# The order of the input projections in a hybrid mLSTM and differential-attention layer

## The chip, the cores and the metric

The kernel runs on one core of a Trainium2 chip, in one launch. The metric is the device time in microseconds (us) of that core. The core's engines work side by side and each runs its own instructions in the order in which the program lists them: TensorE (PE, with its weight loads PEld), VectorE (DVE), ScalarE (ACT), GpSimd (POOL), and SyncE (SP), which here issues the transfers.

## The reference

One decoder layer over 2048 tokens of width 1024, all in float32.

```python
u = rmsnorm(h, attn_norm_g[l])
z = jnp.matmul(u, w_in[l].astype(jnp.float32))
mq, mk, mv, mo, mi, mf, aq, ak, av = split_columns(z)
y_m = mlstm_mixer(mq, mk, mv, mo, mi, mf, ...)      # 4 heads of 128, conv + gates, chunkwise memory
y_a = diff_attn_mixer(aq, ak, av, ...)              # 4 heads, two causal softmax maps per head
h = h + jnp.matmul(jnp.concatenate([y_m, y_a], axis=-1), w_out[l])
u2 = rmsnorm(h, mlp_norm_g[l])
h = h + jnp.matmul(jnp.square(jax.nn.relu(jnp.matmul(u2, w_up[l]))), w_down[l])
gate = jax.nn.sigmoid(jnp.matmul(rmsnorm(h, ple_norm_g[l]), w_ple_gate[l]))
h = h + gate * jnp.matmul(p[l], w_ple_proj[l])
```

Attention is causal, so a query block of 128 tokens needs the keys and values of all blocks before it. The mLSTM memory runs along the sequence, so a part of the sequence can only follow the part before it.

## The kernel before

The sequence is cut into four parts of 512 tokens, numbered j = 0 to 3. `phase1` (the input projections, mLSTM, attention, and the output projection of part 0) is followed by `phase2` (the rest of the layer), whose large buffer `U_r` takes space that phase 1 gives back at its end. Large products are made three times, from a high and a low part of each operand (`mm3`, lines 137 to 139, and `prod`, line 921).

The projections of one part come in two pieces: `z_attn(j)` (six weight groups: values, queries and keys of the four heads, and the gates) and `z_mlstm(j)` (eight weight groups, two a head). Each is 576 matmuls. Here they are called A0 to A3 and M0 to M3. Both read the scaled activations `Uh` and `Ul` of part j, which lie in one buffer, `ubuf`, that holds one part at a time. `make_u(j)` fills it: four loads of x (line 285), four products with the gain (line 297), four splits into high and low (lines 75 and 76). The first time for a part it also makes the row statistics (lines 290, 294, 307). `project` walks through `ORDER` and calls `make_u` whenever the part differs from that of the entry before. A piece's last K blocks leave late: `qk_prep` normalises and rotates (tile `KS_r`, line 749), and `k_out` transposes them on PE (line 756).

Attention is a second stream, one unit for each part, head and block of 128 queries, 64 in all. Unit number i of a head (0 to 15) has i + 1 key blocks, in 1 to 4 chunks of 512 keys. `attn_front` runs two sets, one for each softmax map: scores on PE (784, 787, with the mask 786), row maxima on DVE (788, 792, 793), exponentials on ACT (796); then DVE combines the two maps (808). `attn_back` transposes the result (PE 820, copies on ACT 823 and DVE 825), multiplies by the values (PE 832), and scales it (ACT 835 and 838, DVE 840, POOL 841 and 842); line 499 transposes it back and 500 copies it out. The stream may enter part j only when A(j) is done, and until then it yields:

```python
while j not in done:
    yield 0.0
```

The loop at the end of `phase1` mixes the two streams by hand-set costs: each step of projection work adds a debt of attention work, by what is left of each. A scheduler then orders the instructions once more, so that the order of the built program is not quite that in which the code was written; it stands fixed before the kernel runs.

Of the kernel before, what the change touches and what calls it, by code (L numbers as in the profile page):

```python
# [33 lines left out]
FY = 1.2  # L34
AHEAD = 1
MOVES = [(("z", "s"), ("z", "ta")), (), (("ta", "s"),), (("z", "s"),)]
ORDER = [("a", 0), ("a", 1), ("a", 2), ("m", 0), ("m", 1), ("a", 3), ("m", 2), ("m", 3)]


@with_exitstack  # L40
# [135 lines left out]
def phase1(tc, a, wbuf, ubuf, rbuf, ps, yT, hd, qkdr, vdr, ident, identr, identb, masks, ones, negh, split, rstd_col, spread, acc0):  # L176
    nc = tc.nc
    with ExitStack() as ctx:
# [78 lines left out]
        wseq, wq = [], []  # L257
        for kind, j in ORDER:
            if kind == "a":
# [9 lines left out]
        def u_front(j, tb):  # L269
            if rcol[j] is None:  # L270
                rcol[j] = pc.tile([P, 2, 4], F32, name=f"rcol{j}")
                stats.add(j)
            xk = pu.tile([P, KT, P], F32, tag="xk", name="xk")
            start = j == 0 and tb == 0 and j in stats
            if start:
                for k in range(KT):
                    if k % 4 == 0:
                        nc.sync.dma_start(xk[:, k:k + 4], a["x_in"][0, :, k:k + 4])
                    if k == 0:
                        wq.append(load_w(*wseq.pop(0), True))  # L280
                    nc.scalar.activation(Uh[:, 0, k], xk[:, k], AF.Copy, scale=gcol[:, k:k + 1])  # L281
                    nc.vector.scalar_tensor_tensor(out=Ul[:, 0, k], in0=xk[:, k], scalar=gcol[:, k:k + 1],
                                                   in1=Uh[:, 0, k].bitcast(F32), op0=ALU.mult, op1=ALU.subtract)
            else:
                nc.sync.dma_start(xk, a["x_in"][4 * j + tb])
            acc = None
            if j in stats:
                sq = pu.tile([P, KT, P], F32, tag="sq", name="sq", bufs=1)
                acc = pu.tile([P, P], F32, tag="acc", name="acc", bufs=2)
                nc.scalar.activation(pl(sq), pl(xk), AF.Square)  # L290
                n = KT // 2
                while n:
                    o = sq[:, 0:n] if n > 1 else acc.unsqueeze(1)
                    (nc.gpsimd if j > 0 else nc.vector).tensor_tensor(out=o, in0=sq[:, 0:n], in1=sq[:, n:2 * n], op=ALU.add)
                    n //= 2
            if not start:
                nc.vector.tensor_tensor(out=xk, in0=xk, in1=gB, op=ALU.mult)
            return None if start else xk, acc
# [13 lines left out]
        def make_u(j, fronts):  # L312
            for tb in range(4):
                u_back(j, tb, *(fronts.pop(0) if fronts else u_front(j, tb)))
            stats.discard(j)
# [232 lines left out]
        def project():  # L548
            fronts = []
            for i, (kind, j) in enumerate(ORDER):  # L550
                if i == 0 or j != ORDER[i - 1][1]:
                    make_u(j, fronts)

                def ahead():
                    if i + 1 < len(ORDER) and ORDER[i + 1][1] != j:
                        fronts.extend(u_front(ORDER[i + 1][1], tb) for tb in range(2))

# [663 lines left out]
```

## Time and profile before

| | us |
|---|---|
| median of 3 runs | 3007.65 |
| lowest, highest | 3003.73, 3011.53 |
| profiled execution, device time | 3009.52 |
| its span, first to last instruction | 3007.7 |
| PE busy | 2881.5 |
| DVE, ACT, POOL busy | 1953.8, 1378.4, 1294.6 |

The profiled execution is one of its own; its device time is 1.8 us more than its span. The busy time of PE comes from matmuls that overlap at their ends, so a count of matmuls over a stretch without gaps gives a better price for one than its own duration does. The granted clock (PEclk) is the share of TensorE's full 2.4 GHz; 0.5 is its lower level, 1.2 GHz. Of the span, 0 to 1298 us is phase 1; its pieces begin at 6 (A0), 112 (A1), 242 (A2), 373 (M0), 525 (M1), 709 (A3), 842 (M2), 1034 (M3) and 1226 us (the output projection of part 0).

### The profile page before, as it was taken

To read this page: it belongs to the slowest core of one execution; us is meant where nothing else is said; L and a number is where in the kernel's file an instruction comes from. 1 tells how busy PE (TensorE), PEld (TensorE's weight loads), DVE (VectorE), ACT (ScalarE), POOL (GpSimd) and SP (SyncE) were. 2 spreads that over 40 slices of the span, in tenths; PEclk is the share of its full clock that TensorE was granted. 3 is DMA by queue.
4 is the path that set the end of the run, shared out by engine and by line. 5 is a ranking of instruction groups with operands and counts; after the bars stand their busy time and mean duration, and the time that the engine had idled before them with its cause. 6 is when DMAs were issued, how large, how long until landed. Compare 5 with 4: busy or idle time off the path is not lost.

```text
span 3007.7 us, 43131 instructions
## 1 busy us (share of the span) xinstructions
PE 2881.5 (96%) x15752; PEld 2464.6 (82%) x15752; DVE 1953.8 (65%) x3819; ACT 1378.4 (46%) x3134; POOL 1294.6 (43%) x1012
## 2 busy tenths in 40 slices
PE   7899999898989999999999999999999999999999
PEld 6888988788978788876888888887878888888887
DVE  7788777667776866558556656564486566565653
ACT  4466666667666665644223332252342233322331
POOL 5767543434542332344333333362463333333441
PEclk9899999999999999999999999999999999999999
DMA  5654544334543423351111111124421111111211
GB/s 157 198 165 146 167 137 116 109 102 137 144 124 91 127 76 100 105 167 46 53 56 43 56 57 49 53 73 154 127 63 57 56 43 56 57 48 51 78 50 63
DMA packets 202421, 282.57 MB, mean 94 GB/s; under 512 B 16096, under 2 KB 143584, under 8 KB 198112
## 3 DMA queue, kind: packets, MB, share of 16 engines
q1 hardware_dynamic: 202208, 279.81, 30.8%
q8 instruction: 124, 2.03, 0.3%
q14 instruction: 89, 0.73, 0.1%
HBM read 239.90 MB, written 39.85 MB: 93 GB/s over the span
## 4 chain that ended last, share of the span: by engine, by line
PE 68%; DVE 14%; POOL 5%; DMA 4%; ACT 4%; issue 4%; SPq 0%; POOLq 0%; ACTq 0%; DVEq 0%
PE bank L921 50%; PE bank L137 4%; PE bank L138 3%; PE bank L139 3%; DMA rbuf<-in_w_in_dram 3%; PE bank L832 3%; POOL wbuf L76 2%; DVE PP_r L808 1%; DVE mxp_r L788 1%; PE bank L784 1%; PE bank L787 1%; PE bank L820 1%; DVE qn_r L735 1%; ACT PP_r L796 1%; POOL rn_r L731 1%
## 5 line engine op out<-in xcount | busy, mean ns | idle before, releaser
L76 POOL TENSOR_TENSOR wbuf<-rbuf,wbuf 128x512 fp32r<-128x512 f32 (+2 forms) x632 | 913.5, 1452 | 1339.4 <-ACT wbuf L75 1264.3
L75 ACT ACTIVATE wbuf<-rbuf 128x512 fp32r<-128x512 f32 (+2 forms) x632 | 414.8, 661 | 877.4 <-PE bank L921 593.5
L921 PE MATMUL bank<-U_r,wbuf 128*128 128x512 f32 x2928 | 702.2, 392 | 13.0 <-POOL wbuf L76 4.7
L921 PEld LDWEIGHTS bank<-U_r,wbuf 128*128 128x128 f32 x2928 | 552.2, 189 | 133.0 <-POOL wbuf L76 6.1
L921 PE MATMUL bank<-ubuf,wbuf 128*128 128x512 f32 x2208 | 574.0, 390 | 2.4 <-DVE ubuf L76 1.3
L886 DVE TENSOR_TENSOR h_r<-bank,h_r 128x512 f32<-128x512 f32 x504 | 343.1, 687 | 267.9 <-PE bank L921 266.1
L921 PEld LDWEIGHTS bank<-ubuf,wbuf 128*128 128x128 f32 x2208 | 414.3, 188 | 92.8 <-issue 2.9
L921 PE MATMUL bank<-ybuf,wbuf 128*128 128x512 f32 x1872 | 478.8, 391 | 3.6 <-ACT wbuf L75 2.4
L921 PEld LDWEIGHTS bank<-ybuf,wbuf 128*128 128x128 f32 x1872 | 351.6, 188 | 79.5 <-ACT wbuf L75 3.7
L137 PE MATMUL bank<-wbuf,ubuf 128*128 128x256 f32 (+1 forms) x1280 | 378.8, 296 | 16.0 <-ACT ubuf L281 5.7
L138 PE MATMUL bank<-wbuf,ubuf 128*128 128x256 f32 (+1 forms) x1280 | 371.9, 291 | 0.9 <-DVE wbuf L251 0.9
L139 PE MATMUL bank<-wbuf,ubuf 128*128 128x256 f32 (+1 forms) x1280 | 371.6, 290 | 0.5 <-DVE ubuf L76 0.5
L137 PEld LDWEIGHTS bank<-wbuf,ubuf 128*128 128x128 f32 x1280 | 248.2, 194 | 21.9 <-ACT ubuf L281 5.7
L138 PEld LDWEIGHTS bank<-wbuf,ubuf 128*128 128x128 f32 x1280 | 248.0, 194 | 3.7 <-DVE wbuf L251 1.5
L139 PEld LDWEIGHTS bank<-wbuf,ubuf 128*128 128x128 f32 x1280 | 247.7, 194 | 2.5 <-DVE ubuf L76 0.8
L788 DVE TENSOR_REDUCE mxp_r<-bank 128x1 f32<-128x512 f32 (+3 forms) x320 | 186.5, 602 | 72.9 <-PE bank L787 72.2
L796 ACT ACTIVATE PP_r<-bank,mx_r 128x512 f32<-128x512 f32 (+3 forms) x320 | 196.2, 623 | 59.3 <-DVE mx_r L793 58.2
L832 PE MATMUL bank<-V_r,at_r 128*128 128x128 f32 x1088 | 140.8, 283 | 1.3 <-ACT at_r L823 0.5
L784 PE MATMUL bank<-KT_r,QT_r 128*128 128x512 f32 (+3 forms) x320 | 128.7, 402 | 11.5 <-ACT PP_r L796 7.1
L832 PEld LDWEIGHTS bank<-V_r,at_r 128*128 128x128 f32 x1088 | 134.3, 198 | 3.9 <-DVE at_r L825 1.2
L137 PE MATMUL bank<-ubuf,wbuf 128*128 128x512 f32 x320 | 131.0, 409 | 2.2 <-DVE mx_r L792 0.8
L808 DVE SCALAR_TENSOR_TENSOR PP_r<-PP_r,sc_r 128x512 f32<-128x512 f32 (+3 forms) x160 | 129.8, 858 | 1.2
(285 smaller groups left out, 4278.5 us busy)
## 6 DMA issues: line engine op xcount, KB each, us to landing
rbuf<-in_w_in_dram SPq DMA_DIRECT2D x208, 256.0 KB, 2.9
rbuf<-in_w_down_dram SPq DMA_DIRECT2D x128, 256.0 KB, 2.6
rbuf<-in_w_up_dram SPq DMA_DIRECT2D x32, 1024.0 KB, 4.9
KT_r<-qk_d SPq DMA_DIRECT2D x40, 512.0 KB, 5.3
qk_d<-kst_r SPq DMA_DIRECT2D x64, 256.0 KB, 3.0
QT_r<-qk_d SPq DMA_DIRECT2D x128, 128.0 KB, 3.8
rbuf<-in_w_out_dram SPq DMA_DIRECT2D x32, 512.0 KB, 3.7
rbuf<-in_x_in_dram SPq DMA_DIRECT2D x31, 512.0 KB, 3.9
```

Of the source, the lines that this page charges most:

```text
L75: nc.scalar.activation(hi, raw, AF.Copy)
L76: eng.tensor_tensor(out=lo, in0=raw, in1=hi.bitcast(F32), op=ALU.subtract)
L137: nc.tensor.matmul(ps, lhsT=lh, rhs=rh, start=(start and i == 0), stop=False)
L138: nc.tensor.matmul(ps, lhsT=lh, rhs=rl, start=False, stop=False)
L139: nc.tensor.matmul(ps, lhsT=ll, rhs=rh, start=False, stop=(stop and i == n - 1))
L784: nc.tensor.matmul(Sp[:, 0:n], lhsT=QT[:, 0, m], rhs=rhs, start=True, stop=False)
L788: nc.vector.tensor_reduce(out=mxp[:, m, ci:ci + 1], in_=Sp[:, 0:n], op=ALU.max, axis=AX.X)
L796: nc.scalar.activation(pp[:, 0:n], sps[ci][:, 0:n], AF.Exp, bias=mx[:, m:m + 1], scale=0.125, accum_out=lp[:, m, ci:ci + 1])
L808: nc.vector.scalar_tensor_tensor(out=A[:, 0:n], in0=PP[1][ci][:, 0:n], scalar=sc[:, 0:1], in1=A[:, 0:n], op0=ALU.mult, op1=ALU.add)
L832: nc.tensor.matmul(po, lhsT=ats[kb // 4][:, (kb % 4) * P:(kb % 4 + 1) * P], rhs=VV[kb // 4][:, kb % 4], start=(kb == 0), stop=(kb == i))
L886: eng.tensor_tensor(out=out, in0=x, in1=y, op=op)
L921: nc.tensor.matmul(p, lhsT=l, rhs=r, start=start and i == q == 0, stop=stop and i == n - 1 and q == 2, skip_group_check=on)
```

## The change

One line: the order in which the eight pieces are computed. M0 follows A0 and M1 follows A1, so `make_u` runs 6 times where it ran 8 times: parts 0 and 1 are no longer made a second time. In the built program the loads of x fall from 31 to 23, and the products of line 297 likewise. The weights are loaded piece by piece in either order, the same number of times.

```diff
--- before.py
+++ after.py
@@ -34,7 +34,7 @@
 FY = 1.2
 AHEAD = 1
 MOVES = [(("z", "s"), ("z", "ta")), (), (("ta", "s"),), (("z", "s"),)]
-ORDER = [("a", 0), ("a", 1), ("a", 2), ("m", 0), ("m", 1), ("a", 3), ("m", 2), ("m", 3)]
+ORDER = [("a", 0), ("m", 0), ("a", 1), ("m", 1), ("a", 2), ("a", 3), ("m", 2), ("m", 3)]
 
 
 @with_exitstack
```

The attention stream has its parts 1 and 2 released later: A1 is the third piece in place of the second, A2 the fifth in place of the third. Line 820, one row for each key block of each unit, stands 544 times in PE's order either way. Before, it stands 33, 59, 61, 88, 59, 97 and 116 times within the pieces A1, A2, M0, M1, A3, M2 and M3, and 31 times within the output projection of part 0. In the changed program it stands 40, 4, 66, 34, 59, 76 and 118 times within M0, A1, M1, A2, A3, M2 and M3, 44 times within that output projection, and 103 times behind its last matmul.

PE's order before, where that output projection ends (lines 137 to 139 on `ubuf` and `wbuf`) and phase 2 begins (line 921):

```order
L137 MATMUL bank_68<-ubuf,wbuf 128x512
L138 MATMUL bank_68<-ubuf,wbuf 128x512
L139 MATMUL bank_68<-ubuf,wbuf 128x512
L921 MATMUL bank_70<-ybuf,wbuf 128x512 x7
L921 MATMUL bank_71<-ybuf,wbuf 128x512 x2
L499 MATMUL bank_67<-ident,ya_r 128x128
L921 MATMUL bank_72<-ybuf,wbuf 128x512 x2
L921 MATMUL bank_70<-ubuf,wbuf 128x512 x3
L921 MATMUL bank_72<-ybuf,wbuf 128x512 x7
L921 MATMUL bank_72<-ubuf,wbuf 128x512 x3
```

Before, one row of attention (499) is left behind the last row of the projection.

PE's order in the changed program, from the last two rows of the same output projection on:

```order
L138 MATMUL bank_71<-ubuf,wbuf 128x512
L139 MATMUL bank_71<-ubuf,wbuf 128x512
L921 MATMUL bank_72<-ybuf,wbuf 128x512 x9
L921 MATMUL bank_72<-ubuf,wbuf 128x512 x3
L820 MATMUL bank_67<-ident,PP_r 128x128 x4
L921 MATMUL bank_71<-ybuf,wbuf 128x512 x2
L784 MATMUL bank_66<-KT_r,QT_r 128x512
L787 MATMUL bank_66<-KT_r,QT_r 128x512
L921 MATMUL bank_71<-ybuf,wbuf 128x512 x7
L921 MATMUL bank_71<-ubuf,wbuf 128x512 x3
L784 MATMUL bank_69<-KT_r,QT_r 128x512
```

Scores (784, 787) and transposes (820) now stand behind it, with a few matmuls of phase 2 between them. They go on for some 140 rows, and this is how they end:

```order
L499 MATMUL bank_67<-ident,ya_r 128x128
L820 MATMUL bank_67<-ident,PP_r 128x128 x4
L921 MATMUL bank_70<-ybuf,wbuf 128x512 x9
L921 MATMUL bank_70<-ubuf,wbuf 128x512 x6
L820 MATMUL bank_67<-ident,PP_r 128x128 x7
L832 MATMUL bank_67<-V_r,at_r 128x128 x15
L820 MATMUL bank_67<-ident,PP_r 128x128 x4
L499 MATMUL bank_67<-ident,ya_r 128x128
L820 MATMUL bank_67<-ident,PP_r 128x128 x12
L832 MATMUL bank_67<-V_r,at_r 128x128 x16
L499 MATMUL bank_67<-ident,ya_r 128x128
L921 MATMUL bank_70<-U_r,wbuf 128x512
```

Behind the last row of the output projection stand 80 score matmuls (40 each of lines 784 and 787, ten sets of four chunks), 103 rows each of lines 820 and 832, and 45 of line 921; the first product with `U_r` comes behind the last row 499.

ACT's order in the changed program, in the same stretch (bank_66, 69, 70 and 68 hold the four chunks of one set of scores, bank_67 is the one bank of transposes and outputs):

```order
L835 ACTIVATE ya_r<-bank_67 128x128
L838 ACTIVATE ascr_r,ass_r<-ya_r 128x128
L823 ACTIVATE at_r<-bank_67 128x512
L500 ACTIVATE yo_r<-bank_67,small 128x128
L796 ACTIVATE PP_r,lp_r<-bank_66,mx_r 128x512
L796 ACTIVATE PP_r,lp_r<-bank_69,mx_r 128x512
L796 ACTIVATE PP_r,lp_r<-bank_70,mx_r 128x512
L796 ACTIVATE PP_r,lp_r<-bank_68,mx_r 128x384
L823 ACTIVATE at_r<-bank_67 128x512 x2
L796 ACTIVATE PP_r,lp_r<-bank_66,mx_r 128x512
L796 ACTIVATE PP_r,lp_r<-bank_69,mx_r 128x512
L796 ACTIVATE PP_r,lp_r<-bank_70,mx_r 128x512
```

Two sets of exponentials (796) belong to one unit. Ahead of every second set stand the copies of a finished unit, lines 835, 838, 823 and 500.

DVE's order there (lines 792 and 793 make the bias that a set's exponentials need):

```order
L802 TENSOR_REDUCE ll_r<-lp_r 128x2
L788 TENSOR_REDUCE mxp_r<-bank_70 128x1
L804 RECIPROCAL sc_r<-ll_r 128x1
L839 SCALAR_TENSOR_TENSOR ass_r<-ll_r 128x1
L788 TENSOR_REDUCE mxp_r<-bank_68 128x1
L805 SCALAR_TENSOR_TENSOR sc_r<-ll_r,small,sc_r 128x1
L792 TENSOR_REDUCE mx_r<-mxp_r 128x1
L808 SCALAR_TENSOR_TENSOR PP_r<-PP_r,sc_r 128x512 x3
L808 SCALAR_TENSOR_TENSOR PP_r<-PP_r,sc_r 128x256
L793 TENSOR_SCALAR mx_r<-mx_r 128x1
L825 COPY at_r<-bank_67 128x128
```

The combination of the unit before (808, four chunks) stands between 792 and 793 of the next unit's first set.

## Rows read from the trace of the kernel before

**Rows 1.** The page, busy time, share of the span and instructions.

```profile
PE 2881.5 (96%) x15752; PEld 2464.6 (82%) x15752; DVE 1953.8 (65%) x3819; ACT 1378.4 (46%) x3134; POOL 1294.6 (43%) x1012
```

**Rows 2.** Windows: length, busy time by engine (instructions), granted clock, DMA share, GB/s.

```profile
0.00:1298.00 1298.00, 1198.34 (x8376) 1081.98 (x8377) 935.47 (x2485) 818.49 (x2223) 612.46 (x545) 0.97 0.44 129
1298.00:1384.00 86.00, 71.93 (x280) 52.43 (x279) 69.04 (x76) 43.28 (x69) 45.89 (x26) 0.94 0.40 132
...
1400.00:1500.00 100.00, 100.00 (x443) 82.81 (x442) 60.34 (x83) 26.25 (x44) 33.89 (x25) 1.00 0.17 53
```

**Rows 3.** Windows around the seven changes from one piece to the next.

```profile
106.00:142.00 36.00, 26.79 (x158) 24.09 (x159) 34.45 (x103) 16.15 (x39) 26.72 (x23) 0.72 0.60 179
238.00:278.00 40.00, 32.70 (x213) 29.98 (x212) 32.62 (x88) 24.80 (x70) 31.87 (x31) 0.83 0.47 138
368.00:394.00 26.00, 22.09 (x166) 20.69 (x165) 23.34 (x53) 15.15 (x42) 14.31 (x10) 0.93 0.57 173
522.00:564.00 42.00, 35.78 (x237) 31.48 (x236) 27.91 (x69) 30.87 (x86) 20.55 (x18) 0.92 0.42 125
704.00:756.00 52.00, 44.33 (x321) 41.09 (x321) 36.80 (x96) 36.56 (x101) 24.23 (x25) 0.90 0.44 137
832.00:856.00 24.00, 17.75 (x129) 16.17 (x128) 20.09 (x41) 13.21 (x33) 17.57 (x14) 0.93 0.61 186
1020.00:1050.00 30.00, 24.57 (x173) 20.64 (x172) 25.48 (x52) 19.29 (x52) 10.66 (x9) 1.00 0.66 184
```

**Rows 4.** Waits of PE, 106 to 142 us: total, times, longest.

```profile
PE bank L756 <- DVE KS_r L749: 8.2, 3, 4.1
```

**Rows 5.** Line 297 from 360 to 545 us: ns min/median/max, first and last start.

```profile
L297 DVE TENSOR_TENSOR rbuf<-rbuf,gcol x8: 1210/1221/1743, 368.6 to 542.8; 128x1024 f32<-128x1024 f32 x8
```

**Rows 6.** Timeline of ACT around two sets: start, duration, idle before.

```profile
943.55 0.69 ACT L796 ACTIVATE PP_r<-bank,mx_r 128x512 f32<-128x512 f32 x1
...
951.46 0.68 ACT L796 ACTIVATE PP_r<-bank,mx_r 128x512 f32<-128x512 f32 x1
...
953.44 0.38 ACT L796 ACTIVATE PP_r<-bank,mx_r 128x128 f32<-128x128 f32 x1
...
960.39 0.69 ACT L796 ACTIVATE PP_r<-bank,mx_r 128x512 f32<-128x512 f32 x1 [1.74 <-DVE mx_r L793]
```

**Rows 7.** Timeline of DVE, same unit.

```profile
950.62 0.15 DVE L793 TENSOR_SCALAR mx_r<-mx_r 128x1 f32<-128x1 f32 x1
953.05 1.36 DVE L788 TENSOR_REDUCE mxp_r<-bank 128x1 f32<-128x512 f32 x2 [2.29 <-PE bank L787]
...
955.78 0.15 DVE L792 TENSOR_REDUCE mx_r<-mxp_r 128x1 f32<-128x4 f32 x1
955.90 4.40 DVE L808 SCALAR_TENSOR_TENSOR PP_r<-PP_r,sc_r 128x512 f32<-128x512 f32 x4
960.22 0.14 DVE L793 TENSOR_SCALAR mx_r<-mx_r 128x1 f32<-128x1 f32 x1
```

**Rows 8.** Timeline of PE, same unit.

```profile
952.30 0.48 PE L784 MATMUL bank<-KT_r,QT_r 128*128 128x512 f32 x1
```

**Rows 9.** Lines of PE, 1034 to 1226 us: count, busy us, mean ns, idle before.

```profile
L832 PE MATMUL bank<-V_r,at_r 128*128 128x128 f32 x204 | 24.1, 276 | 0.0
L820 PE MATMUL bank<-ident,PP_r 128*128 128x128 f32 x116 | 18.2, 275 | 3.8 <-ACT ya_r L835 2.4 <-ACT at_r L823 1.4
```

**Rows 10.** Lines of POOL and of ACT, 1150 to 1300 us, by form.

```profile
L842 POOL TENSOR_SCALAR ya_r<-ya_r,ass_r 128x128 f32<-128x128 f32 x6 | 4.1, 684 | 0.5
L841 POOL TENSOR_TENSOR ass_r<-ass_r,negh 128x1 f32<-128x1 f32 x6 | 3.3, 552 | 27.5 <-DVE ass_r L840 20.7 <-DVE mx_r L792 6.6
...
L823 ACT ACTIVATE at_r<-bank 128x512 f32<-128x512 f32 x16 | 9.6, 598 | 8.0 <-PE bank L820 7.9
L500 ACT ACTIVATE yo_r<-bank,small 128x128 f32<-128x128 f32 x5 | 1.9, 374 | 2.8 <-PE bank L499 2.8
```

**Rows 11.** Waits of PE, 1298 to 1384 us.

```profile
PE bank L921 <- ACT wbuf L75: 4.4, 4, 2.0
```

## The prediction

> **What bounds the kernel now.** I read the page first: PE is busy 2881.5 us, 96% of the span, and no other engine is above 65% [rows 1]. So the change can win only what PE loses, by idling or by a lowered clock, and can lose only by making PE idle somewhere else. Next the windows: of the first 1298 us PE is busy 1198, so it idles 100; over the first 86 us of phase 2 it idles 14 [rows 2]. The first of these rows also has a mean granted clock of 0.97. A stretch of length L at clock c loses up to L x (1 - c) of work at 2.4 GHz, here 1298 x 0.03, about 39 us. Idle plus clock, phase 1 loses about 139 us. The reader is to see two things there: this is the whole stock from which a gain can come, and the projections themselves are no cheaper in another order.
>
> Then I looked where the loss lies. In the seven windows around the change from one piece to the next [rows 3], idle plus clock is: A0 to A1 9.2 + 10.1 = 19.3; A1 to A2 7.3 + 6.8 = 14.1; A2 to M0 3.9 + 1.8 = 5.7; M0 to M1 6.2 + 3.4 = 9.6; M1 to A3 7.7 + 5.2 = 12.9; A3 to M2 6.3 + 1.7 = 7.9; M2 to M3 5.4. Together they are 74.9 us, over half of the stock. At each of them the scaled activations are made anew, the late K blocks of an attention piece leave, or both. At the first, 8.2 us of PE's waits are for K blocks from DVE [rows 4], while DVE was busy 34.45 of 36 us [rows 3].
>
> **Term 1, two remakes fewer.** What is removed is eight loads, eight products of 1.2 us on DVE [rows 5] and eight splits. As work on DVE, ACT and POOL it lies beside PE and costs nothing; what it costs is the wait at the boundary. The new order has these seven boundaries: A0 to M0 and A1 to M1 without a remake; M0 to A1 and M1 to A2, both like the old M1 to A3 (12.9 each); A2 to A3, like A1 to A2 (14.1); A3 to M2 (7.9) and M2 to M3 (5.4) as before. For A0 to M0 nothing in the trace is the same: late K blocks and the first attention units, but DVE free of the remake. Its ends are 0 and the 19.3 of A0 to A1; I take 8, the nearest boundary with late K blocks (A3 to M2). For A1 to M1 the ends are 0 and 7.9, and I take 4, half of that. The sum is 65.2 against 74.9: a gain of 9.7, between a gain of 21.7 and a loss of 5.5.
>
> **Term 2, attention that is left over.** A1 and A2 now run with little attention beside them (4 and 34 rows of line 820, where they had 33 and 59), because its next part is not released. The order of the changed program shows where this ends: 103 of the 544 rows stand behind the last projection matmul, where before none stood. PE, which takes its rows in order, then has nothing else to do but 45 matmuls of phase 2. What counts is how long this tail lasts and how much of it PE works.
>
> PE's work in it: 80 score matmuls at 0.226 us (443 matmuls in 100 us without a gap [rows 2]) are 18.1; 103 transposes at 18.2/116 = 0.157 are 16.2; 103 value products, of two records each, at 24.1/102 = 0.236 are 24.3 [rows 9]; 45 matmuls of phase 2 are 10.2. Together 68.8 us.
>
> Its length is a chain. The trace shows one unit of that size, of 1664 to 1792 keys, though with projections between. Four exponentials start 0.66 apart (951.46 to 953.44 [rows 6]); a score matmul starts 0.16 after the first has freed its bank [rows 8], and its maximum 0.75 after that [rows 7]; a maximum takes 0.68, 792 and 793 about 0.3. So a set that waits for nothing else takes 2.64 + 0.16 + 0.75 + 0.68 + 0.3, about 4.6 with a step between engines. In the first set of each unit the combination of the unit before, 4.4 us (from 955.90 to 960.22), stands ahead of line 793: 9.0. Unhindered, a unit takes 13.6; in the trace it took 16.8, from the exponential at 943.55 to the one at 960.39 [rows 6]. In the tail ACT's second set stands behind line 500 of a finished unit, and that waits for 841, 842, a transpose and itself: 0.55 + 0.68 + 0.28 + 0.37 [rows 9, 10], about 2. I take 15.6 a unit. Ten sets are nine steps, 4.5 units, 70 us; 2 us before them; and behind the last set a drain of 3.6 for exponentials and last maximum, 4.4 for the combination, 1.4 for a last transpose and its copy (0.60 [rows 10]), 3.8 for 16 value products, 2.0 to line 500, and some 3 us of steps between engines, my estimate from the gaps in [rows 6, 7]. That is 18, so the tail lasts 90 us, and PE would idle 90 - 69 = 21.
>
> The clock adds to this. In the window from 106 to 142 us PE was busy 74% and the granted clock was 0.72 [rows 3]; the tail would be busy 76%. At 0.72 its work needs 68.8/0.72 = 95.6 us, so PE and the chain would take turns at being late. I take 97 for the tail, a loss of 28. The least I can argue for is 13.6 a unit and no loss of clock: 81 - 69 = 12. The most is the work at 1.2 GHz throughout: 137.6 - 68.8 = 69. The Trainium skill, page "TensorE: Matmul & The Clock Gate", section "Part 1: The HAM clock gate", says that half rate is the default and activity releases it; the trace agrees in kind, 0.72 where PE had gaps and 1.00 where it had none [rows 2, 3].
>
> **Term 3, the start of phase 2.** It loses 14.1 + 86 x 0.06 = 19.2 now [rows 2], 4.4 of it to the split of weights on ACT [rows 11]. Loads and splits that the tail now covers should save that: 4, between 0 and 9. `U_r` still waits for the end of phase 1, so the rest stays.
>
> Inside the pieces I expect no change: A3, M2 and M3 have 59, 76 and 118 rows of line 820 where they had 59, 97 and 116, so attention gets no denser. The rest of phase 2 runs at a clock of 1.00 with PE full and is not touched.
>
> **Sum.** 3009.5 (the profiled execution) - 9.7 + 28 - 4 = 3023.8. That execution is 1.9 above the median of the runs, so I predict 3022.
>
> **Rivals.**
> - *Faster.* The tail is short: only DVE's own work bounds a unit, eight maxima at 0.68, 4.4 for the combination and about 2 for a copy and the small ones, 11.9 us. The tail is then 11.9 x 4.5 + 20 = 74 and loses 5; with the best of term 1, 3009.5 - 21.7 + 5 - 4 - 1.9 = 2987, and with its middle value 2999. For it speaks that no chain runs alone anywhere in the trace; against it, the written order of ACT and DVE. It decides below about 11.8 us a unit. Chance 0.13.
> - *No change.* The boundaries give all they can and the tail loses 22: 3009.5 - 21.7 + 22 - 4 - 1.9 = 3004. Chance 0.17.
> - *The clock stays low through the tail.* PE's work alone takes 137.6 us: 3009.5 - 9.7 + 69 - 4 - 1.9 = 3063. For it speaks the row from 106 to 142 us; against it, that PE has work every few us and the lowest mean in any window of [rows 3] is 0.72. Chance 0.10.
> - *My forecast*, a tail that loses more than the remakes gave, 3010 to 3042: chance 0.60.
>
> That two remakes really go is not in doubt, since the eight loads are missing from the program.
>
> **How the numbers follow.** A measurement of this kernel can tell about 0.3% from no change, 9 us. The forecast lies above that nearly throughout, and so does the low clock: slower 0.70, within 0.3% 0.17, faster 0.13. The range leaves out most of the faster case and the end of the low clock: 2998 to 3054. The forecast's own range is 3010 to 3042.
>
> **What would show it.** In the profile after: between the last row of lines 137 to 139 and the last row 499 some 85 to 105 us, with PE busy under 80% and a clock well under 1; units there 14 to 17 us apart, DVE waiting for scores and ACT for line 793; windows at A0 to M0 and A1 to M1 that lose 12 or less together; `make_u` 6 times. A tail under 75 us, or boundaries that give back 25 or more, would make the prediction wrong.

## The result, and the profile after

The changed kernel takes 3052.32 us (median of 4 runs, 3047.28 to 3060.63) where the kernel before took 3008.03 beside it (3003.73 to 3011.53). The ratio is 1.0151, 95% interval 1.0136 to 1.0166: slower by 44 us. That lies in the range of the prediction (2998 to 3054), but the loss is three times the 14 us that were forecast. The profiled execution of after is its fastest, 3047.28 us; it stands 37.8 above the profiled one of before, and the ledger below is made against that.

First the page of the changed kernel, then its windows. The windows show four stages (to the last projection matmul, to the last row 499, here called the tail, then the start of phase 2, and the rest), then the seven changes between pieces, then the tail in parts; the columns are as in [rows 2, 3].

```profile
span 3045.5 us, 43117 instructions
PE 2891.6 (95%) x15752; PEld 2474.3 (81%) x15752; DVE 1952.8 (64%) x3805; ACT 1374.4 (45%) x3126; POOL 1285.5 (42%) x1010
```

```profile
0.00:1225.40 1225.40, 1130.77 (x7970) 1027.55 (x7971) 886.24 (x2347) 767.64 (x2080) 594.55 (x528) 0.98 0.44 131
1225.40:1342.00 116.60, 86.10 (x453) 67.60 (x451) 52.10 (x128) 48.83 (x139) 13.08 (x18) 0.87 0.16 50
1342.00:1420.00 78.00, 58.82 (x226) 45.60 (x225) 61.92 (x70) 39.64 (x63) 40.50 (x23) 0.87 0.35 115
1420.00:3045.50 1625.50, 1615.94 (x7106) 1333.55 (x7106) 952.55 (x1262) 518.27 (x844) 637.36 (x442) 1.00 0.20 64
...
104.00:140.00 36.00, 31.35 (x219) 28.34 (x219) 29.65 (x91) 14.96 (x44) 18.70 (x19) 0.95 0.54 156
250.00:280.00 30.00, 24.31 (x172) 23.14 (x172) 16.49 (x39) 17.90 (x44) 24.07 (x19) 0.83 0.37 119
345.00:372.00 27.00, 23.66 (x195) 22.39 (x194) 22.14 (x66) 16.33 (x45) 15.76 (x15) 1.00 0.50 147
500.00:545.00 45.00, 40.32 (x303) 37.85 (x302) 34.51 (x89) 30.78 (x84) 29.38 (x26) 0.92 0.47 132
625.00:680.00 55.00, 45.65 (x317) 40.60 (x315) 45.77 (x112) 34.70 (x87) 30.04 (x28) 0.94 0.49 151
765.00:790.00 25.00, 20.09 (x149) 19.10 (x149) 24.00 (x50) 14.21 (x35) 16.74 (x12) 0.86 0.73 238
930.00:970.00 40.00, 36.16 (x253) 32.46 (x251) 27.70 (x62) 27.74 (x79) 14.07 (x12) 0.91 0.45 128
...
1300.00:1320.00 20.00, 15.04 (x66) 12.46 (x66) 7.83 (x20) 8.19 (x23) 1.18 (x2) 0.74 0.00 1
1320.00:1342.00 22.00, 14.45 (x83) 12.13 (x83) 1.57 (x4) 3.52 (x10) 2.36 (x4) 0.77 0.00 0
```

In the second row the reader sees the cost: for 116.6 us no engine is nearly full, PE is busy 86.1 at a granted clock of 0.87, and DVE, ACT and POOL less than half of the time. No engine bounds this stretch; a chain does. The rows of the boundaries answer to [rows 3], and their sum is lower than it was. In the tail's last 42 us the mean granted clock is 0.74 and 0.77, a mix of the two levels.

**A ledger by length.** PE's busy time is modelled at the ends of matmuls, so the stages are better compared by length, with the prediction's prices for the work that has moved. Each side is one profiled execution, and executions of one kernel lie some 10 us apart (after: 3047 to 3061), so differences of a few us are not safe. Attention behind the last projection matmul is 18.1 + 16.2 + 24.3 = 58.6 us of PE's work, the 45 matmuls of phase 2 there 10.2.

| | before | after | difference | forecast |
|---|---|---|---|---|
| to the last projection matmul, and the attention left over | 1298.4 | 1225.4 + 58.6 = 1284.0 | -14.4 | term 1: -9.7 |
| tail, less PE's work in it | 0 | 116.7 - 68.8 = 47.9 | +47.9 | term 2: +28 |
| phase 2 with all its matmuls | 1709.3 | 1703.4 + 10.2 = 1713.6 | +4.3 | term 3: -4 |
| span | 3007.7 | 3045.5 | +37.8 | +14.3 |

The new order does make the projections cheaper, by somewhat more than was forecast. The tail takes that three times over.

**What paces the tail.** The timeline of PE in the changed kernel, two units and the end; the bracket says how long PE had idled and for whom:

```profile
1285.64 4.80 PE L832 MATMUL bank<-V_r,at_r 128*128 128x128 f32 x26 [2.34 <-DVE at_r L825]
1290.20 0.48 PE L784 MATMUL bank<-KT_r,QT_r 128*128 128x512 f32 x1
...
1301.70 5.90 PE L832 MATMUL bank<-V_r,at_r 128*128 128x128 f32 x28 [2.42 <-DVE at_r L825]
1307.35 0.48 PE L784 MATMUL bank<-KT_r,QT_r 128*128 128x512 f32 x1
...
1321.25 3.62 PE L832 MATMUL bank<-V_r,at_r 128*128 128x128 f32 x30 [0.72 <-DVE at_r L825]
1325.28 0.66 PE L820 MATMUL bank<-ident,PP_r 128*128 128x128 f32 x4 [0.42 <-ACT ya_r L835]
1327.27 0.34 PE L499 MATMUL bank<-ident,ya_r 128*128 128x128 f32 x1 [1.33 <-POOL ya_r L842]
1328.07 1.11 PE L820 MATMUL bank<-ident,PP_r 128*128 128x128 f32 x4 [0.46 <-ACT yo_r L500]
1329.87 1.11 PE L820 MATMUL bank<-ident,PP_r 128*128 128x128 f32 x4 [0.69 <-ACT at_r L823]
1331.67 1.12 PE L820 MATMUL bank<-ident,PP_r 128*128 128x128 f32 x4 [0.69 <-ACT at_r L823]
1333.63 5.77 PE L832 MATMUL bank<-V_r,at_r 128*128 128x128 f32 x32 [0.84 <-DVE at_r L825]
1341.80 0.33 PE L499 MATMUL bank<-ident,ya_r 128*128 128x128 f32 x1 [2.41 <-POOL ya_r L842]
```

And DVE there:

```profile
1230.74 0.69 DVE L788 TENSOR_REDUCE mxp_r<-bank 128x1 f32<-128x512 f32 x1 [1.97 <-PE bank L787]
...
1298.64 2.61 DVE L808 SCALAR_TENSOR_TENSOR PP_r<-PP_r,sc_r 128x512 f32<-128x512 f32 x4
1301.16 0.15 DVE L793 TENSOR_SCALAR mx_r<-mx_r 128x1 f32<-128x1 f32 x1
1301.22 0.42 DVE L825 COPY at_r<-bank 128x256 f32<-128x256 f32 x1
1308.10 0.69 DVE L788 TENSOR_REDUCE mxp_r<-bank 128x1 f32<-128x512 f32 x1 [6.46 <-PE bank L787]
```

The circle is not the one of the forecast. DVE's copy 825 of one unit stands behind the combination of the next (808 until 1301.16), PE waits 2.42 us for it, then makes that unit's value products, 5.90 us at a granted clock of 0.50 (from 1301.7 to 1307.0; as many products took 3.29 from 1239.64, at 1.00), and only behind these stand the next scores (1307.35), for whose maxima DVE has meanwhile idled 6.46. The scores that follow such products begin 17.2 us apart (1290.20 and 1307.35). The last rows show the drain: PE's transposes pass through one bank, each waiting for the copy of the one before, first for the unit before the last, then for the last.

### The profile page after: what moved, and what is told of

It reads as the page before. It is cut to its first block, busy times and chain, and to the rows that moved or that the text cites. A ratio compares the mean times of both kernels' runs of the same rounds, so it can differ in the third digit from the quotient of the medians.

```text
span 3045.5 us, 43117 instructions
## 1 busy us (share of the span) xinstructions
PE 2891.6 (95%) x15752; PEld 2474.3 (81%) x15752; DVE 1952.8 (64%) x3805; ACT 1374.4 (45%) x3126; POOL 1285.5 (42%) x1010
## 4 chain that ended last, share of the span: by engine, by line
PE 51%; DVE 3%; ACT 1%; issue 0%; DMA 0%; SPq 0%; POOL 0%; DVEq 0%; ACTq 0%
PE bank L921 51%; DVE U_r L76 1%; DVE tmp_r L886 0%; DVE rbuf L886 0%; DVE tmp_r L1002 0%; PE bank L92 0%; DMA h_r<-h_d 0%; DVE U_r L1002 0%; DVE pre L1002 0%; ACT wbuf L75 0%; DVE h_r L886 0%; DVE acc L90 0%; DVE pre L886 0%; DVE ubuf L76 0%; DVE wbuf L76 0%
## 5 line engine op out<-in xcount | busy, mean ns | idle before, releaser
L137 PE MATMUL bank<-wbuf,ubuf 128*128 128x256 f32 (+1 forms) x1280 | 378.3, 296 | 15.3 <-ACT ubuf L281 5.7
L796 ACT ACTIVATE PP_r<-bank,mx_r 128x512 f32<-128x512 f32 (+3 forms) x320 | 195.9, 621 | 65.2 <-DVE mx_r L793 61.3
L832 PEld LDWEIGHTS bank<-V_r,at_r 128*128 128x128 f32 x1088 | 140.7, 206 | 14.8 <-DVE at_r L825 12.0
L841 POOL TENSOR_TENSOR ass_r<-ass_r,negh 128x1 f32<-128x1 f32 x64 | 39.9, 624 | 252.0 <-DVE ass_r L840 224.0
```

The source lines that it names most:

```text
L137: nc.tensor.matmul(ps, lhsT=lh, rhs=rh, start=(start and i == 0), stop=False)
L796: nc.scalar.activation(pp[:, 0:n], sps[ci][:, 0:n], AF.Exp, bias=mx[:, m:m + 1], scale=0.125, accum_out=lp[:, m, ci:ci + 1])
L832: nc.tensor.matmul(po, lhsT=ats[kb // 4][:, (kb % 4) * P:(kb % 4 + 1) * P], rhs=VV[kb // 4][:, kb % 4], start=(kb == 0), stop=(kb == i))
L841: nc.gpsimd.tensor_tensor(out=ss[:, 0:1], in0=ss[:, 0:1], in1=negh, op=ALU.pow)
```

## The experiments

### The order alone, without a tail

Both orders with less attention, so that nothing is left over in either (`e9_before_cut` and `e10_after_cut`, the same edit):

```diff
-        units = [(j, h, tb) for j in range(NT1) for h in range(NH) for tb in range(4)]
+        units = [(j, h, tb) for j in range(NT1) for h in range(NH if j < 3 else 1) for tb in range(4)]
```

> The kernel before, without the attention of heads 1, 2 and 3 of part 3 (12 of 64 units; zeros are stored for them). Left out are 174 rows each of lines 820 and 832 and 192 score matmuls, some 111 us of PE by the prices of the prediction, so 2894 us, between 2870 and 2915, if PE stays the bound. It is there to be compared with the next kernel.

> The changed kernel with the same 12 units left out, on the PSUM banks as they were. In the built order no attention row stands behind the last projection, so there is no tail. Theory A (the order itself gains, the tail loses): 5 to 20 us faster than the kernel before with the same cut. Rival B (late attention costs as much inside the pieces): slower than it by 10 us or more. Rival D (remakes were free, the tail alone is the change): the same within 5 us.

Measured: 2905.17 us in the order before (2901.5 to 2908.53), 2879.46 in the new one (2878.82 to 2882.79); to the uncut kernel before, ratios of 0.9662 (0.9647 to 0.9676) and 0.9579 (0.9564 to 0.9593). Windows of the cut kernel before, then of the cut kernel after, each to its last projection matmul:

```profile
0.00:1197.70 1197.70, 1086.39 (x7629) 987.27 (x7630) 854.19 (x2231) 733.30 (x1955) 601.31 (x521) 0.97 0.45 133
1197.70:2899.70 1702.00, 1680.44 (x7375) 1384.41 (x7373) 1016.60 (x1327) 556.00 (x903) 683.63 (x467) 0.99 0.21 65
```

```profile
0.00:1177.80 1177.80, 1081.82 (x7629) 986.79 (x7630) 822.46 (x2215) 725.34 (x1946) 586.86 (x519) 0.97 0.44 131
1177.80:2881.00 1703.20, 1682.89 (x7374) 1385.47 (x7372) 1017.66 (x1330) 556.68 (x905) 682.76 (x467) 0.99 0.21 65
```

With no tail the new order is faster: 26 us by the medians, more than the 5 to 20 expected, and 19.9 in phase 1 by the profiled executions, with phase 2 within 1.2 us. So the order loses nothing by itself here, though with a third less attention to place; for the full kernel the ledger says the same: its loss stands in the row of the tail.

### More and less left over

Three kernels with the banks as they were. `e5_after_eight_makes` calls `make_u` at every piece of the new order; `e8_four_makes_old_banks` has A and M of each part side by side; `e6_seven_makes` puts only M0 ahead.

```diff
-                if i == 0 or j != ORDER[i - 1][1]:
+                if True:
```

```diff
+ORDER = [("a", 0), ("m", 0), ("a", 1), ("m", 1), ("a", 2), ("m", 2), ("a", 3), ("m", 3)]
```

```diff
+ORDER = [("a", 0), ("m", 0), ("a", 1), ("a", 2), ("a", 3), ("m", 1), ("m", 2), ("m", 3)]
```

In these texts the fourth kernel is `e4_four_makes`, and in the next section the first kernel is `e1_after_two_ta`.

> The new order, with the scaled activations made anew at every piece, 8 times as before the change. In the built order 120 rows of line 820 and 50 score pairs stand behind the last projection (103 and 40 in the changed kernel). Theory A: two boundaries cost some 10 to 15 us again, and the tail, a unit longer, some 8 more: 3073 us, between 3060 and 3085. Rival D (remakes are free): 3052 to 3062 us.

> The order with 4 makes of the fourth kernel, on the PSUM banks of the kernel before. 120 rows of line 820 and 50 score pairs stand behind the last projection (103 and 40 in the changed kernel), so the tail is more than a unit longer. Theory A: some 10 us won at boundaries and some 10 lost in the tail, 3052 us, between 3040 and 3065: the gain of the fourth kernel is then from having no tail. Rival E (the gain of the fourth kernel comes from two makes fewer): under 3020 us.

> Order A0, M0, A1, A2, A3, M1, M2, M3 with the banks as before: seven makes, 70 rows of line 820 and 20 pairs of scores behind the last projection (changed kernel: 103 and 40). Theory that the tail of left-over attention is what costs, by its length: 20 pairs fewer are 2.5 units of 16 us, 40 us shorter, with 21 us less work of PE in it, so 19 us less loss, and 2 us more for the seventh make: 3035 us, with a tail of about 75 us. Rival, that the cost is the drain and the low clock behind the last projection, whatever is left over: 3050 or more.

Measured: 3065.12 us (ratio 1.0198, 1.0176 to 1.0220), 3043.08 (1.0122, 1.0104 to 1.0141) and 3047.31 (1.0127, 1.0110 to 1.0144). The tail's window in each, in that order:

```profile
1218.90:1360.00 141.10, 103.79 (x552) 80.80 (x550) 61.98 (x153) 58.87 (x170) 17.36 (x21) 0.87 0.20 55
```

```profile
1191.20:1337.00 145.80, 106.90 (x552) 83.95 (x550) 62.66 (x154) 59.37 (x170) 16.60 (x21) 0.83 0.20 53
```

```profile
1269.60:1345.90 76.30, 57.57 (x313) 46.09 (x311) 27.47 (x66) 29.15 (x81) 10.59 (x12) 0.87 0.11 36
```

The ledger by length for these, each with its own left-over rows at the same prices. A pair is one score chunk (a row 784 and a row 787) behind the last projection matmul:

| | makes | pairs left | projections with the attention left over | tail less its work | phase 2 |
|---|---|---|---|---|---|
| before | 8 | 0 | 1298.4 | 0 | 1709.3 |
| seven makes | 7 | 20 | 1269.6 + 37.5 = 1307.1 | 76.3 - 47.7 = 28.6 | 1710.9 |
| after | 6 | 40 | 1225.4 + 58.6 = 1284.0 | 116.7 - 68.8 = 47.9 | 1713.6 |
| after, eight makes | 8 | 50 | 1218.9 + 72.6 = 1291.5 | 141.1 - 82.8 = 58.3 | 1711.9 |
| four makes | 4 | 50 | 1191.2 + 72.6 = 1263.8 | 145.8 - 82.8 = 63.0 | 1710.9 |

Eight makes and four makes came within their expected ranges. The loss in the tail follows what is left over: about 9 us, and 1.0 us for each pair (28.6 at 20 pairs, 47.9 at 40, 58 to 63 at 50). The seven makes had their tail of 75 and lost 28.6 there, where 29 was expected, but missed the expected total by 12 us: by the ledger their projections became 8.7 dearer than before instead of cheaper. Why was not followed up. With eight makes the new order still gains 6.9 in the projections; so by these single executions two remakes are worth 7.5 of the 14.4, and the rest is where the boundaries fall. (The medians of e5 and of the changed kernel differ by 12.8 us, these two executions by 16.2.) The four makes gain most of all in the projections, 34.6, and lose it to the longest tail.

### Banks in place of a tail

The tail exists because attention, which yields while A1 and A2 are late, then doesn't catch up. From part 2 on its transposes and outputs pass through one PSUM bank (`ta`); with a second one kept (e3, e4, e11) or given back (e1), no row 820 is left over. The line `MOVES` says which bank goes to whom when the attention of a part begins (its third and fourth entries belong to the parts of A2 and A3); `z` are the banks of the projections, `m` the two of the mLSTM, `s` those of the scores.

In `e1_after_two_ta` (new order) and `e2_before_two_ta` (order before):

```diff
-MOVES = [(("z", "s"), ("z", "ta")), (), (("ta", "s"),), (("z", "s"),)]
+MOVES = [(("z", "s"), ("z", "ta")), (), (("ta", "s"),), (("z", "s"), ("m", "ta"))]
```

In `e3_after_keep_ta`:

```diff
+MOVES = [(("z", "s"), ("z", "ta")), (), (("z", "s"),), (("m", "s"),)]
```

In `e4_four_makes` (the order of four makes), `e11_after_given_banks` (new order) and `e12_before_given_banks` (order before):

```diff
+MOVES = [(("z", "s"), ("z", "ta")), (), (("z", "s"), ("m", "s")), ()]
```

> The new order, and in attention part 3 one PSUM bank goes from the mLSTM's ring to the ring of transposes and outputs, which then has two. In the built order no attention row stands behind the last projection matmul any more (103 rows of line 820 in the changed kernel). Theory A (the loss is the tail; up to the last projection the new order is 15 us better): no tail, the start of phase 2 as before the change, 2994 us, between 2985 and 3003, faster than the kernel before. Rival B (attention released late costs as much inside the pieces as behind them, the tail only shows it): M2 and M3 stall instead, 3020 to 3050 us.

> The same bank move in the order of the kernel before, which has no tail. Theory A: nothing to win, 3008 us, between 2998 and 3016. Rival C (the bank move is worth as much in any order, and the order has nothing to do with it): 10 us or more faster than before, under 2998.

> The new order, where transposes and outputs keep two banks from part 2 on (scores take theirs from the projections in part 2 and from the mLSTM in part 3). No row of attention behind the last projection, and 92, 118 and 171 rows of line 820 in A3, M2 and M3. Theory A: as the first kernel, 2985 to 3003 us. Rival B: 3020 to 3050 us.

> Attention and mLSTM of each part next to each other, so that the scaled activations are made 4 times, with scores taking a bank each from projections and mLSTM in part 2, so that no attention row stands behind the last projection. Theory A: two boundaries more without a remake, some 15 us better than the first kernel, 2980 us, between 2968 and 2995. Rival B (attention part 3, released only before M3, crowds into it and stalls): 3000 us or more.

> The order of the changed kernel with the banks of the kernel of four makes (a z bank and an m bank given to the attention's scores in part 3). Theory that four makes matter only because with them the m bank is taken when one mLSTM piece is left: here M2 and M3 both run with it gone, so some rows of the mLSTM stand behind the last projection, and the time is near that of the other two versions with an m bank given, 3030 us (3022 to 3040). Rival, that the banks alone make the gain: 2999 us or less, like the four makes. Rival, that the remakes count for most: 3010 to 3020, since there are two more of them than in the four makes.

> The order of the kernel before with the same banks. Theory (a lack of m banks behind the remakes): 3040 us, as with the other gift of an m bank in this order (3044), and some 10 slower than the same banks in the changed order. Rival, that the banks alone make the four makes faster than before: under 3000 us, in both orders alike.

| | median us | ratio to before, 95% interval | last projection matmul ends | from there to the end |
|---|---|---|---|---|
| before, beside e1 to e4 and beside e11 and e12 | 3004.91, 3006.98 | 1 | 1298.4 | 1709.3 |
| e1, new order | 3034.32 | 1.0096 (1.0081 to 1.0111) | 1317.3 | 1718.3 |
| e2, order before | 3044.21 | 1.0128 (1.0113 to 1.0143) | 1316.7 | 1719.7 |
| e3, new order | 3031.03 | 1.0089 (1.0073 to 1.0106) | 1300.5 | 1721.3 |
| e4, four makes | 2998.75 | 0.9982 (0.9973 to 0.9992) | 1286.1 | 1708.5 |
| e11, new order | 3027.28 | 1.0066 (1.0051 to 1.0081) | 1298.6 | 1727.1 |
| e12, order before | 3110.24 | 1.0346 (1.0331 to 1.0362) | 1384.1 | 1724.8 |

None of these has a row 820 behind the last projection matmul. The expectations for e1, e2 and e3 (2994, 3008 and 2994 us) missed, and e4 gained less than its 2980. An explanation from the built order and the last two columns, argued and not tested by itself: the `m` bank is not free. The mLSTM then lags, and in all but e4 its last rows (674, 684, 686, 715) stand behind the projections, so that phase 2 starts late: from there to the end these five take 9 to 18 us more than before. That is all of the loss of e11, whose projections end where those of before do. The projections of e1, e3 and e11 also end later than the 1284.0 of the changed kernel with its attention. With equal banks the new order is faster than the old one, by 10 us (e1 to e2) and 83 (e11 to e12). The gap of e12 was far larger than expected. In its order A2 is done early, the attention of part 2 begins near the end of M0 (its first row 820 runs at 502 us), and M1, M2 and M3 run on one `m` bank, in e11 only M2 and M3. A `z` bank goes at the same time; which of the two costs the 83 was not tested. Its waits of PE from 300 us on (total, times, longest) name the mLSTM first, but with 18 us they are only a part of the 86 by which phase 1 is longer; the rest was not followed up:

```profile
PE bank L715 <- DVE og_r L708: 18.1, 10, 6.1
```

e11 answers for the four makes: the banks alone don't do it (3027), nor does the order of four makes alone (3043). Together they take all rows but one 499 off the tail and end the projections 12.3 us earlier than before, of the 34.6 that the ledger gave this order with its old banks. That kernel is the one that beats before, by 0.2%:

```profile
0.00:1286.10 1286.10, 1190.84 (x8376) 1075.76 (x8377) 916.23 (x2459) 805.69 (x2208) 587.07 (x538) 0.98 0.42 124
1286.10:2994.60 1708.50, 1684.61 (x7377) 1384.96 (x7376) 1017.02 (x1334) 558.74 (x911) 680.09 (x468) 0.99 0.21 67
```

### The chain within the tail

`e7_copy_on_act` takes the copy 825 from behind the combination:

```diff
-        if ci % 4 < 3:
+        if True:
             nc.scalar.activation(at[:, :n], pt[:, :n], AF.Copy)
```

> The changed kernel with the fourth copy of every unit on ScalarE too (line 825 never runs, line 823 for all). Theory that a unit of the tail is paced by value products that stand ahead of the next scores and wait for a copy which stands behind the combination on VectorE (PE waits 2.3 us for it in three units): units 2 us shorter in the tail, 14 for 16, and PE's waits there for ScalarE no longer than 1 us; about 10 us less in the tail, 3043 us, and the three boundaries of the projections where VectorE is full lose no more. Rival, that the time goes to ScalarE's own queue instead (each copy is 0.6 us there, behind four exponentials): 3052 to 3065.

Measured: 3050.08 us, ratio 1.0142 (1.0122 to 1.0161), no gain that can be told from the 1.0151 of after. PE in the tail of this kernel:

```profile
1268.06 0.48 PE L784 MATMUL bank<-KT_r,QT_r 128*128 128x512 f32 x1
...
1280.25 5.72 PE L832 MATMUL bank<-V_r,at_r 128*128 128x128 f32 x32 [0.69 <-ACT at_r L823]
1285.73 0.48 PE L784 MATMUL bank<-KT_r,QT_r 128*128 128x512 f32 x1
...
1294.76 3.17 PE L832 MATMUL bank<-V_r,at_r 128*128 128x128 f32 x26 [0.37 <-ACT at_r L823]
...
1297.68 0.48 PE L784 MATMUL bank<-KT_r,QT_r 128*128 128x512 f32 x1
...
1308.23 4.95 PE L832 MATMUL bank<-V_r,at_r 128*128 128x128 f32 x28 [0.47 <-ACT at_r L823]
...
1312.94 0.48 PE L784 MATMUL bank<-KT_r,QT_r 128*128 128x512 f32 x1
```

The wait of 2.3 to 2.4 us ahead of the value products is gone (0.37 to 0.69), and the same two units are 12.0 and 15.3 us apart where they were 15.5 and 17.2. But the two units before them became longer: the products of one took 5.72 us at a granted clock of 0.50, and the unit 17.7 where it had 14.6. From 1248.67 to 1312.94 four units take 16.1 us each, and in the changed kernel 16.2. So the wait is rightly read, but it did not set the mean pace. In both kernels the short units have short value products ahead of their scores and the long units long ones (3.17 us and 12.0, 3.84 and 14.6; 5.72 and 17.7, 5.90 and 17.2), and in the two longer units of e7 groups of four transposes ran at the low clock as well, 1.1 us each where they take 0.6 to 0.7 at the full one. And 43 pairs are left over in place of 40, the drain is as long (35 us from the last set's maxima at 1313.7 to the end of the last row 499), the tail's mean clock is 0.84 in place of 0.87, and the tail is 124.4.

### Phase 2's matmuls in the tail, and its start

Behind the last row 499 the changed kernel waits for `U_r`; before, it did not. PE's waits in the changed kernel, in the tail and behind it:

```profile
PE bank L832 <- DVE at_r L825: 8.6, 5, 2.4
PE bank L820 <- ACT at_r L823: 4.8, 7, 0.7
...
PE bank L921 <- ACT U_r L75: 6.6, 1, 6.6
```

SP's queue shows why: the store of the last unit goes first, and the loads for `U_r` 2.2 us behind it.

```profile
1342.57 0.33 SPq L502 DMA_DIRECT2D yT_d<-yo_r  x1
1344.75 1.27 SPq L995 DMA_DIRECT2D tmp_r<-yT_d  x3
```

Before, 34 rows of line 921 that need no `U_r` still ran there by the trace (33 in the expectations). Were they the cover, and is it their running in the tail that makes the drain long? `e13_after_no_late` and `e14_before_no_late`, then `e15_after_late_first` and `e16_before_late_first`:

```diff
-                Y = load_y(0, 1)
+                Y = load_y(0, 1, 0, 5)
+                Y = Y + Y[:3]
```

```diff
-                prod(p, wload8(a["w_out"][m]), y)
+                w = wload8(a["w_out"][m])
+                prod(p, w[5:] + w[:5], y[5:] + y[:5])
```

> The changed kernel, with the last three of the eight blocks of y not loaded for the output projection of part 1: blocks 0 to 2 stand in their place, so three loads and splits into U_r are left out and part of the product is of other data. Behind the last unit nothing is loaded any more before PE can go on, and 96 matmuls of phase 2 stand ahead of the last row 499 where 45 stood. Theory that the 45 matmuls which fill the tail were the cover of that load: no wait of PE for U_r, the start of phase 2 loses 10 to 14 us where it lost 26.5, and the 51 matmuls more (11.5 us) go into idle time of the tail: about 3027 us (3020 to 3040). Rival, that the start loses by the low clock and the splits of weights: 3045 or more.

> The same left out of the kernel before. Theory: the load was covered there by 33 matmuls, so little changes, 3003 to 3009 us, and the difference between the two orders falls from 44 to about 20 us. Rival: the load costs both alike, this one falls by as much as the changed kernel, and the difference stays above 35.

> The changed kernel, with the late blocks (5 to 7 of 8) first in each product of that output projection, so that no matmul of phase 2 can run before U_r is there; the sum is taken in another order, nothing is left out. Theory that the matmuls in front of the last transposes lengthen the drain: the tail is about 6 us shorter (111 for 117), and the 45 matmuls then run behind it, 10 us: 3056 us. Rival, that the chain alone sets the tail: 117 as before, 3062. Rival, that they are all of what the drain is longer than forecast, 16 us: a tail of 101 and 3046.

> The kernel before, with the late blocks (5 to 7 of 8) first in each product of the output projection of part 1, so that none of its matmuls can run before U_r is there. Theory that in the kernel before some 33 matmuls, 7.5 us, cover the loads that stand on SP behind the last store: a wait of PE for U_r of 6 to 8 us appears, as in the changed kernel, and the time is 3013 to 3018 us. Rival, that the start of phase 2 waits for something else, the splits of weights on ScalarE: 3008, within 0.2%, since these go on meanwhile and are then ahead.

Measured: e13 3044.75 us, ratio 1.0128 (1.0103 to 1.0153); e14 3000.65, 0.9976 (0.9966 to 0.9986); e15 3062.09, 1.0182 (1.0145 to 1.0218); e16 3008.84, 1.0006 (0.9997 to 1.0015). Windows of the tail in e13 and in e15, then the first PE behind the last row 499 in e13 and in e16:

```profile
1231.80:1362.40 130.60, 102.53 (x503) 80.82 (x502) 52.71 (x128) 53.00 (x143) 22.89 (x22) 0.83 0.19 57
```

```profile
1226.70:1346.40 119.70, 84.19 (x407) 65.39 (x405) 52.00 (x128) 49.15 (x139) 13.00 (x18) 0.76 0.16 49
```

```profile
1362.06 0.33 PE L499 MATMUL bank<-ident,ya_r 128*128 128x128 f32 x1 [2.35 <-POOL ya_r L842]
1370.15 4.21 PE L921 MATMUL bank<-ybuf,wbuf 128*128 128x512 f32 x9 [7.77 <-DVE h_r L886]
```

```profile
1303.77 2.50 PE L921 MATMUL bank<-U_r,wbuf 128*128 128x512 f32 x5 [8.42 <-ACT U_r L75]
```

My theory of the cover holds for the wait and falls for the time. In e16 the wait appears as forecast, 8.42 us, but the kernel is no slower: 1.4 us and within the interval, where 5 to 10 were expected, as the rival said. PE has fewer gaps later: its other waits up to 1400 us come to 6.4, before to 13.8; phase 2 takes 1711.2 from the last projection matmul, before 1709.3. In e13 the wait for `U_r` is gone and one of 7.77 for line 886 stands in its place, since the loads of `h_r` are on SP behind the same store. Nor did the 51 matmuls more go into idle time of the tail, where I had expected them: it lasts 130.6 us, 14 more than 116.7, at a mean clock of 0.83. e13 came out 8 us under the changed kernel by the medians, but the two intervals overlap; e14 fell by 7, clear of its interval. Their difference stayed 44, so the rival expected rightly. Where the 7 us of e14 come from was not found: its phase 1 is 7.9 shorter, and nothing was changed there but the loads left out at its end; that of e16 is 3.2 shorter with nothing changed in it.

In e15 the tail, with no matmul of phase 2 in it, lasts 119.7 us (1226.7 to 1346.4), not less than 116.7, and its drain 33.4 in place of 34.0. The rival that the chain alone sets the tail had 117 and 3062. So the 45 matmuls lengthen neither. That is a net result: without them the tail's granted clock is 0.76 in place of 0.87, so what they take from the chain and what they do for the clock is not told apart. That there is room for 45 doesn't make room for 96, as e13 shows.

## Why the prediction was right in sign and wrong in size

- **What bounds the kernel**: right. The gain came from what PE loses at the boundaries, the loss from where PE idles and is clocked down.
- **Term 1**: right in mechanism, somewhat low. Forecast 9.7, measured 14.4 in the full kernel; 19.9 to 26 with the attention cut. Idle and clock by boundary (forecast behind the bar): A0 to M0 4.7 + 1.8 = 6.5 | 8; M0 to A1 10.8 | 12.9; A1 to M1 3.3 | 4; M1 to A2 8.3 | 12.9; A2 to A3 12.7 | 14.1; A3 to M2 8.4 | 7.9; M2 to M3 7.4 | 5.4. Together 57.4 against 65.2 forecast and 74.9 before [rows 3]. The two without a remake lose 9.8 together, under the 12 that I had set as the test.
- **Term 2** is the step that failed: that a tail of chained units would cost more than the remakes gave was right, its size was not, 47.9 in place of 28. PE's work in the tail was right (68.8 forecast; 86.10 busy, less up to 15.4 of clock, is 70.7). Its length was not: 116.7 in place of 97. By parts, forecast without the clock and measured: the start 2 and 5.3 (1225.4 to the maximum at 1230.74); nine steps 70 and 77.4 (to 1308.10), 15.6 and 17.2 a unit; **the drain 18 and 34.0**. The drain is 16 of the 26.7 missing, of which I had put 7 down to the clock without saying where. I had counted from the last set on one combination, one last transpose and one set of value products. In the trace the combination ends at 1317.6, the unit before the last still has its transposes and products (to 1325.28, 7.7 us), and then the last unit's four groups of transposes go one behind the other through the one bank (8.4 us to 1333.63, for which I had 1.4), and its products take 5.8 at a low clock where I had 3.8. That one bank is the reason is read from PE's waits there; no run had a tail with two.
- **The pace of a unit** came out near the forecast (17.2, a little over the expected 14 to 17) for another reason than given, so this nearness is luck. The combination took 2.3 to 2.7 us, not the 4.4 of [rows 7], and ACT's line 500 was not what counted: the exponentials began some 0.4 us behind line 793. What did, by the trace, were the value products of another unit ahead of the next scores, at either clock, and the wait ahead of them; e7 took the wait away and left the mean pace as it was. In the first of these units PE also waited 2.6 us for keys (`KT_r`), which no term had.
- **Term 3**: forecast -4, measured +4.3. Over all kernels with the old banks and all of the attention phase 2 takes 1706 to 1715 us by length, so this term is nothing within some 4 us. Its reason was wrong: work that moved into the tail was not saved behind it. PE waits there 6.6 us for `U_r`, whose loads stand behind the last store, but e16, where such a wait cost no time, leaves open whether that is the cause.
- **The clock** fell, but not as in the rival: the tail's mean is 0.87, above 0.72 of the first row of [rows 3], and it costs up to 15.4 of the 116.7. The Trainium skill, page "TensorE: Matmul & The Clock Gate", section "Part 1: The HAM clock gate", has half rate as the default, which activity releases. The trace agrees in kind: 1.00 where phase 2 runs nearly without gaps, 0.74 and 0.77 in the tail's last 42 us, where PE is busy 75% and 66% of the time.
- **The rival on the other side** (faster, below 11.8 us a unit) did not come: the mean was 17.2. The gain that it hoped for from the boundaries, 10 to 22 us, is there once no tail is: 20 to 26 in the cut kernels, 14 in the ledger. The rival of no change had the tail lose 22; it lost 48.

## What to carry to other kernels

Work that an order leaves behind the last dense stage costs the length of its chain, not its instructions: here, beyond PE's own work in it, some 9 us and 1.0 us for each score chunk, with DVE, ACT and POOL less than half busy, and three times what the better order had saved. When you price such a tail, walk the pipeline's drain unit by unit, with every stage that is still in flight and every buffer that it has only once; that was the step that I cut short. And a wait that the trace names at a seam, such as the one for `U_r`, is not yet a cost: put it in or take it out, as e16 did with 8.4 us of it, and see whether the time follows.

## What the runs showed of the hardware that was not expected

The combination of four chunks (line 808) took 2.34 to 2.74 us in the tail and 4.40 in [rows 7]. In the kernel before, POOL ran two splits of weights within that combination's 4.40 us:

```profile
956.46 3.03 POOL L76 TENSOR_TENSOR wbuf<-rbuf,wbuf 128x512 fp32r<-128x512 f32 x2 [5.54 <-ACT wbuf L75]
```

In the tail POOL is busy 13.08 of 116.6 us, and not at all beside the combination from 1298.64. The whole trace of the kernel before says the same. Of its instructions of line 808 on 512 elements, 65 have no POOL instruction beside them and took 0.73 to 0.75 us; 15 lie wholly beside POOL's instructions and took 0.74 to 1.79, 1.68 in the median. The row maxima of line 788, which read a PSUM bank, took 0.67 to 0.69 in either case. So a duration read beside a busy POOL can overstate the same instruction in a stretch where POOL rests; that POOL is the cause was not tested by itself.

Within one tail the same number of value products went at two speeds: 28 records in 3.29 us (from 1239.64, granted clock 1.00) and in 5.90 (from 1301.70, 0.50), 0.12 a record against 0.21; before, 204 records took 24.1 us, 0.12 each [rows 9]. PE had stood for 2.42 us just before the slow ones.
